# The last weight chunk of an MLP rounded ahead of the last relu: two buffers, two sums and one tile shape moved at the end of a transformer layer

## The chip, the cores and the metric

The kernel runs on one core of a Trainium2 chip. The metric is the time of one execution on the device in microseconds; the median of several runs is compared. The core's engines each work through a queue of their own: PE (matrix products; PEld is its loading of the stationary operand), DVE (elementwise, vector), ACT (elementwise, scalar), POOL, and SP, which here only issues transfers.

## The reference

One layer over a sequence of 256 rows of width 1024, in fp32: a gated sum of a convolution branch and a sparse attention branch, a cross attention over 256 memory rows, and a squared-relu MLP with hidden width 4096; then a last normalization. What the change touches is the MLP and the end:

```python
    hf = _rmsnorm(h, norm_ffn_g[l]) @ w_ff1[l]
    h = h + jnp.square(jax.nn.relu(hf)) @ w_ff2[l]
return _rmsnorm(h, norm_final_g)
```

## The kernel before

**Precision.** Each fp32 operand of a product is split into a rounded high part and a low part (`hi`, `lo`; of the hidden activations `fs` holds both), and a product is three matmuls: high by high, high by low, low by high (`mm3`). ACT makes the high part of a weight (`act(hi, raw)`, L254), DVE the low part (`raw - hi`, recorded under L79 as every DVE and PE instruction is, because a helper counts them).

**The stream of weights.** All weights come as chunks of 1 MB, in one order, into three rotating `raw` buffers, issued by SP. A chunk is rounded in two halves. Each half takes a slot of the pools `highs` and `lows`, six of each. The functions `split_high` and `split_low` take the next half off a list of jobs; `held` says how many slots stay free. `weights(...)` returns the parts of a half and counts its slot as used. Tiles of 8 KB per partition come from another rotation, `t8`, of 12 buffers. The name `raw66` means chunk 66 of the stream, `hi82_0` the high part of the first half of chunk 82.

**The MLP.** Both weight matrices are cut into 16 chunks of 256 hidden features, `f1` and `f2`. A turn c of the main loop computes both 128-feature tiles of hidden chunk c + 2 (`first`, into a bank `ps_f`), and between them adds chunk c to the output sums (`half_of`, `seventh`, into banks `ps_p`). There are 8 banks. Two are reserved for `ps_f`, but one of these holds a long-lived output sum, so that `ps_f` has a single bank: a new `first` waits until the last one's bank is read.

**Two tile shapes.** In a wide `first` a high weight part meets the high and low activations in one matmul of 512 columns, and the bank ends up with two halves that have to be added: ACT copies one (L396), DVE adds the other (`ft<-ps_f,ft`), ACT applies the relu and the square. A narrow `first` has three matmuls of 256 columns for each step instead; ACT's relu reads the bank directly (L1148), then comes the square (L1153). The turns in `SEVEN` are narrow, the other ones wide. After the square ACT makes the high part of the activations (L1172, `fs`) and DVE the low part.

**Seven banks.** For chunks 0 to 12 (`JOINED` = 13) the output products go through a scheme with seven sums, banks "1" to "7", which are combined into the residual `h_rm` at the end (`add_to` and the instructions on `comb`). Chunks 13 to 15 are multiplied in the ordinary way in `last_products`, which reuses the banks "2", "3", "1", "4", "5" in that order: first row block 0, both halves of the columns, then row block 1. Each is followed by the residual, squares and the last normalization, which scales and stores.

**Order.** The order of instructions in every queue is the order in which the Python code emits them. The end of the code after the loop: the last two parts of chunk 12 (`outer`, `inner`), the two tiles of hidden chunk 15, the weights of `f2` 13 to 15 (chunks 78 to 82 of the stream among others; 82 is `f2` 15, the last), the sums, the last products.

Of the kernel before, what the change touches and what calls it, by code (L numbers as in the profile page):

```python
# [9 lines left out]
F32R = mybir.dt.float32r  # L10
# [6 lines left out]
P = 128  # L17
# [38 lines left out]
N_CHUNK = KT * S  # L56
# [3 lines left out]
SEVEN = (2, 3, 4, 6, 7, 8, 10, 11, 12)  # L60
# [53 lines left out]
def block_kernel(ctx, tc, x, xt, mem, memt, wst, wki, vecs, convw, gout, out):  # L114
# [9 lines left out]
    highs = ctx.enter_context(tc.tile_pool(name="highs", bufs=HALVES))  # L124
    lows = ctx.enter_context(tc.tile_pool(name="lows", bufs=HALVES))
# [4 lines left out]
    def t8(name, dt=F32, shape=(P, KT, S)):  # L130
        return big.tile(list(shape), dt, tag="t8", bufs=12, name=name)

    def parts_t8(name, nkt=KT):
        return Parts([t8(f"{name}{c}", F32R, (P, 4, 2, S)) for c in range(nkt // 4)])

    def w2(name, dt=F32, shape=(P, 512)):
        return work.tile(list(shape), dt, tag="w2", bufs=8, name=name)
# [4 lines left out]
    def ps_mm(name):  # L142
        return bank("mm", 2, name)
# [12 lines left out]
        return (ps_mm if mm_turn[0] % 2 else ps_acc)(name)  # L156


    prepared, whole = {}, {}
    nload = [0]  # L160
    high_jobs, low_jobs = [], []

    def load(parts=1):
        if nload[0] >= len(STREAM):
            return
        c = nload[0]
        nload[0] += 1
        key = STREAM[c]
        raw = t8(f"raw{c}", F32, (P, N_CHUNK)) if c in EARLY else raws.tile([P, N_CHUNK], F32, tag="raw", name=f"raw{c}")
        n = KT * NK if key[0] == "ki" else N_CHUNK  # L170
        src = wki if key[0] == "ki" else wst[INDEX[key]]
        for q in range(parts):
            ns = slice(q * n // parts, (q + 1) * n // parts)
            nc.sync.dma_start(raw[:, ns], src[:, ns])
        if key in WHOLE:
            whole[key] = raw.rearrange("p (k n) -> p k n", k=2 * KT)
            return
        if key[0] == "f2" and key[1] in SEVEN:
            jobs = seven(key, c, raw)
        else:  # L180
            parts = 1 if key[0] == "ki" else 2
            jobs = []
            for q in range(parts):
                ns = slice(q * n // parts, (q + 1) * n // parts)
                jobs.append(Stage((*key, q), lambda ns=ns, q=q, last=q == parts - 1: high(key, c, raw, ns, q, last)))
        if key[0] == "f2" and key[1] < JOINED:

            at = [j.key for j in high_jobs].index(("f1", key[1] + 2, 1))
            first = len(jobs) // 2
            high_jobs[at:at] = jobs[:first]  # L190
            jobs = jobs[first:]
        if key == ("f1", JOINED + 2):

            at = [j.key for j in high_jobs].index(("f2", JOINED - 1, "inner"))
            high_jobs[at:at] = jobs[:1]
            jobs = jobs[1:]
        high_jobs.extend(jobs)

    class Stage:

        def __init__(self, key, high, before=None, slot=True):
            self.key, self.high, self.before, self.slot = key, high, before, slot

        def prepare(self):
            if self.before:
                self.before()
                self.before = None
# [41 lines left out]

    def high(key, c, raw, ns, q, last):  # L250
        n = ns.stop - ns.start
        hi = highs.tile([P, N_CHUNK // 2], F32R, tag="hi", name=f"hi{c}_{q}")[:, :n]
        lo = lows.tile([P, N_CHUNK // 2], F32R, tag="lo", name=f"lo{c}_{q}")[:, :n]
        act(hi, raw[:, ns], AF.Copy)  # L254

        def low():
            dve.tensor_tensor(out=lo, in0=raw[:, ns], in1=hi.bitcast(F32), op=ALU.subtract)
            prepared[(*key, q)] = (hi, lo)
            if last and c not in EARLY:
                load()  # L260

        low_jobs.append(low)

    def split_high():
        if high_jobs and (not high_jobs[0].slot or nsplit[0] - nused[0] < HALVES - held[0]):
            job = high_jobs.pop(0)
            nsplit[0] += job.slot
            job.prepare()
            job.high()

    def split_low():
        if low_jobs:
            low_jobs.pop(0)()
        if len(high_jobs) > 1:
            high_jobs[1].prepare()

    nsplit, nused, held = [0], [0], [1]

    def weights(kind, i, half, kt):

        key = (kind, i, half)
        while key not in prepared:
            split_high()
            split_low()
        nused[0] += half not in ("outer", "inner")
        return [w if kt is None else w.rearrange("p (k n) -> p k n", k=kt) for w in prepared.pop(key)]


# [6 lines left out]
    def add_some():  # L295
        if added and added[0][0] in ready and pe.total >= add_next[0]:
            pair, pause = added.pop(0)
            add_next[0] = pe.total + pause
            ready[pair]()
            if pair not in [p for p, _ in added]:  # L300
                held_back.append((pe.total + 10000, pair))
        if held_back and pe.total >= held_back[0][0]:
            fill.extend(queues.pop(held_back.pop(0)[1]))

    def split_ahead():
        split_low()
        split_high()

    def tick():
        for c in list(chains):  # L310
            if next(c, "end") == "end":
                chains.remove(c)
        while (len(fill) > 1 or (fill and (len(done) > 5 or nused[0] < 5))) and dve.total < pe.total - 1000:
            fill_one()
        dve.total = max(dve.total, pe.total - 2000)
        add_some()

    def fill_one():

        some = [q for q in fill[:3] if q is not turn[0]] or fill  # L320
        q = some[0] if len(some[0]) < 10 and len(fill) > 3 else max(some, key=len)
        turn[0] = q
        q.pop(0)()
        if not q:
            fill.remove(q)
# [99 lines left out]
    for parts in (2, 2, 1):  # L425
        load(parts)
# [8 lines left out]
    half = cst.tile([P, 2], F32, name="half")  # L435
# [336 lines left out]
    parts = (slice(0, P), slice(P, 3 * P))  # L772
# [42 lines left out]
    def qk(name):  # L815
        return big.tile([P, 2, S], F32, tag="qk", bufs=4, name=name)

    for i in range(4):
        q, k = qk(f"q{i}"), qk(f"k{i}")
# [275 lines left out]
    f2 = parts_t8("ff_p")  # L1095
# [112 lines left out]
    def product(name, a, w, j, cs=slice(0, 512)):  # L1208
        if name not in banks:
            banks[name] = {"2": ps_acc, "3": ps_acc, "4": ps_acc, "5": ps_acc, "7": ps_mm}.get(name, ps_aux)(f"ps_p{name}")  # L1210
        used[name] = used.get(name, 0) + 1
        mm3(banks[name], *a, w[0][:, j, cs], w[1][:, j, cs], used[name] == 1, used[name] == uses[name])
# [19 lines left out]
    def seventh(x, name):  # L1232
        w = weights("f2", x.c, name, None)
        split_ahead()
        for j, (bank_name, part) in enumerate(TERMS[name]):
            product(bank_name, x.of(part), w, j)

    def first(x, side, wide):
        ps = ps_mm(f"ps_f{x.c}{side}")
        w = weights("f1", x.c, side, KT)  # L1240
        split_ahead()
        tile_b(ps, w, f2, wide=wide)
        x.after(side, ps if wide else ps[:, :S])
        tick()
        if wide:
            tick()
# [4 lines left out]
    def by_tiles(ap):  # L1251
        return ap.rearrange("p (k f) -> p k f", f=P)
# [29 lines left out]
    def add_to(rb, hf, ps, scales):  # L1282
        h = h_rm[:, 4 * hf : 4 * hf + 4, rb, :]
        dve.scalar_tensor_tensor(out=h, in0=by_tiles(ps), scalar=scales[:, rb : rb + 1], in1=h, op0=ALU.mult, op1=ALU.add)

    for c in range(JOINED):
        hidden.append(Hidden(c + 2))
        x, later = hidden[c], hidden[c + 2]
        first(later, 0, c not in SEVEN)
        x.done()  # L1290
        if c in (0, 1, JOINED - 1):
            split_ahead()
        half_of(x, 0)
        first(later, 1, c not in SEVEN)
        if c < JOINED - 1:
            half_of(x, 1)
    hg = t8("hg", F32, (P, 2, D))
# [5 lines left out]
    r, b = r2[0], banks  # L1303
    minus = small.tile([P, 2], F32, tag="minus", name="minus")
    dve.tensor_scalar(minus, r, -1.0, None, ALU.mult)
    v, e, g = (w2(f"comb{j}") for j in range(3))
    act(v, b["1"], AF.Copy)
    add_to(0, 0, b["2"], r)
    seventh(x, "inner")
    tick()  # L1310
    first(hidden[-1], 1, False)
    held[0] = 0
    ws = {}
    for c in range(JOINED, 16):
        for k in range(2):
            ws[c, k] = weights("f2", c, k, 1)
            split_high()
            tick()
        hidden[c].done()

# [3 lines left out]
            mm3(ps, *hidden[c].row(k, rb), w[0][:, 0, cols], w[1][:, 0, cols], c == JOINED and k == 0,  # L1324
                c == 15 and k == 1)

    add_to(0, 0, v, r)
    add_to(0, 1, b["3"], r)
    dve.tensor_tensor(out=v, in0=b["6"], in1=v, op=ALU.subtract)
    dve.tensor_tensor(out=e, in0=b["5"], in1=v, op=ALU.add)  # L1330
    add_to(0, 1, e, r)
# [92 lines left out]
```

## Time and profile before

| what | value |
|---|---|
| median of 3 runs | 510.51 us (509.75 to 510.89) |
| profiled execution | 510.7 us, span 508.9 us |
| busy in the span | PE 496.6 us, DVE 456.3 us, ACT 348.6 us, POOL 31.6 us |
| mean granted clock of PE | 0.993 |
| largest groups in the chain that ended last | PE 71%, DVE 14%, ACT 5%, DMA 5% |

The profiled execution's own time is 1.8 us above its span. Starts in the rows are microseconds from the span's start. A row of the timeline has start, duration, engine, line, operation and tiles; "x2" joins rows that follow each other; in brackets stands how long the engine had been idle and what ended it. PE's durations overlap, since matmuls are pipelined: its pace is the distance between starts.

### The profile page before, as it was taken

To read this page: it belongs to the slowest core of one execution; us is meant where nothing else is said; L and a number is where in the kernel's file an instruction comes from. 1 tells how busy PE (TensorE), PEld (TensorE's weight loads), DVE (VectorE), ACT (ScalarE), POOL (GpSimd) and SP (SyncE) were. 2 spreads that over 40 slices of the span, in tenths; PEclk is the share of its full clock that TensorE was granted. 3 is DMA by queue.
4 is the path that set the end of the run, shared out by engine and by line. 5 is a ranking of instruction groups with operands and counts; after the bars stand their busy time and mean duration, and the time that the engine had idled before them with its cause. 6 is when DMAs were issued, how large, how long until landed. Compare 5 with 4: busy or idle time off the path is not lost.

```text
span 508.9 us, 8226 instructions
## 1 busy us (share of the span) xinstructions
PE 496.6 (98%) x3090; PEld 443.8 (87%) x3090; DVE 456.3 (90%) x855; ACT 348.6 (69%) x641; POOL 31.6 (6%) x49
## 2 busy tenths in 40 slices
PE   7999999999999999999999999999999999999984
PEld 6999998888888888888898999988988899899964
DVE  5999999999999799999899986799998999799693
ACT  7667777878666667678657666687777777677712
POOL 2002212311211000000000000000000000000000
PEclk9999999999999999999999999999999999999988
DMA  8959678899788524426645654446877445456302
GB/s 319 376 181 276 189 205 247 220 258 272 226 249 243 191 83 167 161 95 241 248 166 176 213 191 131 156 170 184 199 203 297 183 173 175 171 182 243 143 2 83
DMA packets 26649, 100.36 MB, mean 197 GB/s; under 512 B 10592, under 2 KB 11488, under 8 KB 16112
## 3 DMA queue, kind: packets, MB, share of 16 engines
q1 hardware_dynamic: 22544, 92.90, 52.9%
q0 software_dynamic: 3632, 6.59, 7.3%
q8 instruction: 24, 0.39, 0.3%
q10 hardware_dynamic: 432, 0.33, 0.2%
q14 instruction: 17, 0.14, 0.1%
HBM read 91.16 MB, written 1.05 MB: 181 GB/s over the span
## 4 chain that ended last, share of the span: by engine, by line
PE 71%; DVE 14%; ACT 5%; DMA 5%; issue 3%; SPq 0%; POOLq 0%; POOL 0%; DVEq 0%; ACTq 0%
PE ps_f L79 11%; PE ps_conv L79 9%; PE ps_p L79 7%; DMA raw<-in_wst_dram 5%; PE ps_ao L79 4%; PE ps_q L79 4%; PE ps_k L79 4%; PE ps_ga L79 4%; PE ps_gc L79 4%; DVE lo L79 4%; PE ps_v L79 4%; PE ps_xo L79 3%; PE ps_qi L79 2%; PE ps_xk L79 2%; PE ps_xv L79 2%
## 5 line engine op out<-in xcount | busy, mean ns | idle before, releaser
L79 DVE TENSOR_TENSOR lo<-raw,hi 128x1024 fp32r<-128x1024 f32 x145 | 175.7, 1216 | 5.8 <-ACT hi L254 5.7
L254 ACT ACTIVATE hi<-raw 128x1024 fp32r<-128x1024 f32 x145 | 150.7, 1046 | 3.2 <-DMA raw<-in_wst_dram 3.2
L79 PE MATMUL ps_f<-ff_p,hi 128*128 128x256 f32 (+1 forms) x416 | 92.9, 310 | 0.8 <-DVE ft L79 0.8
L79 DVE SCALAR_TENSOR_TENSOR acc<-u,cw,acc 128x234 f32<-128x234 f32 (+29 forms) x190 | 78.2, 464 | 0.3
L79 PEld LDWEIGHTS ps_f<-ff_p,hi 128*128 128x128 f32 x416 | 68.7, 191 | 7.2 <-DVE ft L79 1.6
L79 PE MATMUL ps_f<-ff_p,lo 128*128 128x256 f32 x256 | 70.2, 282 | 0.0
L79 PEld LDWEIGHTS ps_f<-ff_p,lo 128*128 128x128 f32 x256 | 48.7, 190 | 0.9
L79 PE MATMUL ps_conv<-n_p,hi 128*128 128x256 f32 x224 | 41.0, 285 | 0.0
L79 PE MATMUL ps_p<-hi,fs 128*128 128x512 f32 (+1 forms) x124 | 38.4, 381 | 0.6 <-DVE h_rm L79 0.6
L79 PEld LDWEIGHTS ps_conv<-n_p,hi 128*128 128x128 f32 x224 | 34.9, 192 | 0.8 <-issue 0.7
L79 PE MATMUL ps_conv<-n_p,lo 128*128 128x256 f32 x112 | 31.7, 283 | 0.0
L579 POOL DMA_DIRECT2D acc<-products x25 | 21.6, 864 | 122.3 <-ACT products L578 54.8
L79 PEld LDWEIGHTS ps_p<-hi,fs 128*128 128x128 f32 x124 | 23.3, 195 | 5.0 <-DVE h_rm L79 1.0
L79 PE MATMUL ps_p<-lo,fs 128*128 128x512 f32 (+1 forms) x62 | 23.8, 383 | 1.0 <-DVE lo L79 1.0
L79 PE MATMUL ps_q<-n_p,hi 128*128 128x512 f32 x64 | 23.6, 406 | 0.0
L79 PE MATMUL ps_k<-n_p,hi 128*128 128x512 f32 x64 | 23.5, 407 | 0.0
L79 PE MATMUL ps_ao<-o_p,hi 128*128 128x512 f32 x64 | 22.6, 401 | 0.0
L79 PE MATMUL ps_co<-u_p,hi 128*128 128x512 f32 (+1 forms) x80 | 22.2, 351 | 0.0
L79 PE MATMUL ps_mix<-mix_p,hi 128*128 128x512 f32 (+1 forms) x80 | 22.2, 351 | 0.0
L79 PE MATMUL ps_ga<-n_p,hi 128*128 128x512 f32 x64 | 22.0, 396 | 0.0
L79 PE MATMUL ps_gc<-n_p,hi 128*128 128x512 f32 x64 | 22.0, 396 | 0.0
L578 ACT ACTIVATE products<-u,cw 128x231 f32<-128x231 f32 (+24 forms) x50 | 21.9, 489 | 0.0
(370 smaller groups left out, 1194.6 us busy)
## 6 DMA issues: line engine op xcount, KB each, us to landing
raw<-in_wst_dram SPq DMA_DIRECT2D x80, 1024.0 KB, 5.0
acc<-products POOLq DMA_DIRECT2D x25, 256.0 KB, 5.6
raw<-in_wst_dram SPq DMA_DIRECT2D x4, 512.0 KB, 7.3
x_rm<-in_x_dram SPq DMA_DIRECT2D x2, 512.0 KB, 4.1
mem_rm<-in_mem_dram SPq DMA_DIRECT2D x1, 1024.0 KB, 9.1
mem_t<-in_memt_dram SPq DMA_DIRECT2D x1, 1024.0 KB, 11.0
h_t<-in_xt_dram SPq DMA_DIRECT2D x1, 1024.0 KB, 7.1
h_rm<-turned SPq DMA_DIRECT2D x16, 64.0 KB, 7.0
```

The lines of the kernel that those rows point to most:

```text
L79: return fn(*args, **kwargs)
L254: act(hi, raw[:, ns], AF.Copy)
L578: act(prod[:, a, s:], u[:, t, : S - s], AF.Copy, scale=cw[:, t, TAPS - 1 - s : TAPS - s])
L579: nc.gpsimd.dma_start(acc[:, ts, :], prod, accum_op=ALU.add)
```

## The change

Three edits, all in the MLP.

1. The two halves of the last chunk (`f2` 15) no longer take slots: high and low part of a half share one `t8` tile, `both82_0` and `both82_1`. With that the limit `held` needs no lifting, and two calls of `split_ahead` before the last `first` round them earlier.
2. Of the sums that combine the seven banks, two move up: the one of bank "3" and the one of `v`, the copy of bank "1", are added to `h_rm` before the last `first` is emitted.
3. Turn 5 of the main loop uses narrow tiles (hidden chunk 7).

```diff
-                jobs.append(Stage((*key, q), lambda ...: high(key, c, raw, ns, q, last)))
+                jobs.append(Stage((*key, q), lambda ...: high(key, c, raw, ns, q, last),
+                                  slot=key != ("f2", 15)))
...
+            if not slot:
+                elsewhere.add(key)
...
-        hi = highs.tile([P, N_CHUNK // 2], F32R, tag="hi", name=f"hi{c}_{q}")[:, :n]
-        lo = lows.tile([P, N_CHUNK // 2], F32R, tag="lo", name=f"lo{c}_{q}")[:, :n]
+        if (*key, q) in elsewhere:
+            both = t8(f"both{c}_{q}", F32R, (P, 2, n))
+            hi, lo = both[:, 0, :], both[:, 1, :]
+        else:
+            hi = highs.tile([P, N_CHUNK // 2], F32R, tag="hi", name=f"hi{c}_{q}")[:, :n]
+            lo = lows.tile([P, N_CHUNK // 2], F32R, tag="lo", name=f"lo{c}_{q}")[:, :n]
...
-        nused[0] += half not in ("outer", "inner")
+        nused[0] += key not in elsewhere
...
-        first(later, 0, c not in SEVEN)
+        wide = c not in SEVEN and c != 5
+        first(later, 0, wide)
...
-        first(later, 1, c not in SEVEN)
+        first(later, 1, wide)
...
     add_to(0, 0, b["2"], r)
     seventh(x, "inner")
+    add_to(0, 1, b["3"], r)
+    split_ahead()
     tick()
+    add_to(0, 0, v, r)
+    split_ahead()
     first(hidden[-1], 1, False)
-    held[0] = 0
     ws = {}
     for c in range(JOINED, 16):
         for k in range(2):
             ws[c, k] = weights("f2", c, k, 1)
-            split_high()
             tick()
...
-    add_to(0, 0, v, r)
-    add_to(0, 1, b["3"], r)
```

What it does to the queues shows at three places. ACT at the end, before, with what each instruction waits for: `comb0` is `v`, `ft15` and `fs15` are the last hidden chunk, `ps_f151` its second tile.

```order
L1307 ACTIVATE comb0_5354<-ps_p1_4117 128x512
L1172 ACTIVATE fs15_5307<-ft15_5308 128x256 [waits Activation_49]
L254 ACTIVATE hi82_0_5368<-raw82_5266 128x1024 [waits DMAHW5_49,DVE_49]
L1148 ACTIVATE ft15_5308<-ps_f151_5367 128x256 [waits PE_49]
L1153 ACTIVATE ft15_5308<-ft15_5308 128x256 [waits Activation_49]
L254 ACTIVATE hi82_1_5398<-raw82_5266 128x1024 [waits DVE_49]
L1172 ACTIVATE fs15_5307<-ft15_5308 128x256 [waits Activation_49]
```

And now:

```order
L1315 ACTIVATE comb0_5366<-ps_p1_4117 128x512
L261 ACTIVATE both82_0_5372<-raw82_5278 128x1024 [waits DMAHW5_49]
L261 ACTIVATE both82_1_5382<-raw82_5278 128x1024
L1179 ACTIVATE fs15_5319<-ft15_5320 128x256 [waits Activation_49]
L1155 ACTIVATE ft15_5320<-ps_f151_5387 128x256 [waits PE_49]
L1160 ACTIVATE ft15_5320<-ft15_5320 128x256 [waits Activation_49]
L1179 ACTIVATE fs15_5319<-ft15_5320 128x256 [waits Activation_49]
```

Both high parts of chunk 82 stand ahead of the last relu, and neither waits for DVE; the second one stood between the last square and the last `fs`.

DVE at the same place, before: `ps_p2` is bank "2", `lo81_1` the low part of the half before the last two.

```order
L79 SCALAR_TENSOR_TENSOR h_rm<-ps_p_3880,ms_ff,h_rm 128x4x128
L79 TENSOR_TENSOR lo_1_5323<-raw_5253,hi_1_5322 128x1024
L79 TENSOR_TENSOR fs_5307<-ft_5308,fs_5307 128x256 x2
L79 TENSOR_TENSOR lo_0_5369<-raw_5266,hi_0_5368 128x1024
L79 TENSOR_TENSOR lo_1_5399<-raw_5266,hi_1_5398 128x1024
L79 SCALAR_TENSOR_TENSOR h_rm<-comb_5354,ms_ff,h_rm 128x4x128
L79 SCALAR_TENSOR_TENSOR h_rm<-ps_p_3903,ms_ff,h_rm 128x4x128
L79 TENSOR_TENSOR comb_5354<-ps_p_4196,comb_5354 128x512
```

And now:

```order
L79 SCALAR_TENSOR_TENSOR h_rm<-ps_p_3880,ms_ff,h_rm 128x4x128
L79 TENSOR_TENSOR lo_1_5335<-raw_5265,hi_1_5334 128x1024
L79 SCALAR_TENSOR_TENSOR h_rm<-ps_p_3903,ms_ff,h_rm 128x4x128
L79 TENSOR_TENSOR both_0_5372<-raw_5278,both_0_5372 128x1024
L79 SCALAR_TENSOR_TENSOR h_rm<-comb_5366,ms_ff,h_rm 128x4x128
L79 TENSOR_TENSOR both_1_5382<-raw_5278,both_1_5382 128x1024
L79 TENSOR_TENSOR fs_5319<-ft_5320,fs_5319 128x256 x2
L79 TENSOR_TENSOR comb_5366<-ps_p_4196,comb_5366 128x512
```

Four instructions, two low parts and two sums, moved from behind the last two `fs` to ahead of them; the rest keeps its order.

ACT in turn 5, before: `ft7` and `fs7` are hidden chunk 7, `ps_f70` and `ps_f71` its two tiles.

```order
L235 ACTIVATE hi66left_4446<-raw66_4411 128x1024
L396 ACTIVATE ft7_4443<-ps_f70_4444 128x256
L235 ACTIVATE hi66last_4468<-raw66_4411 128x512
L1152 ACTIVATE ft7_4443<-ft7_4443 128x256
L1153 ACTIVATE ft7_4443<-ft7_4443 128x256
```

And now:

```order
L238 ACTIVATE hi66left_4446<-raw66_4411 128x1024
L1155 ACTIVATE ft7_4443<-ps_f70_4444 128x256
L1160 ACTIVATE ft7_4443<-ft7_4443 128x256
L238 ACTIVATE hi66last_4476<-raw66_4411 128x512
L1179 ACTIVATE fs7_4442<-ft7_4443 128x128
```

The relu now reads the bank itself, at the place where the copy stood, behind `hi66left`; on DVE the two instructions `ft7<-ps_f..,ft7` of turn 5 are gone. The transfers that SP issues keep their order.

More of the change, by code (lines that the diff above doesn't have):

```diff
@@ L156, in ps_turn @@
         return (ps_mm if mm_turn[0] % 2 else ps_acc)(name)
-    prepared, whole = {}, {}
+    prepared, whole, elsewhere = {}, {}, set()
     nload = [0]
@@ L184, in load @@
                 ns = slice(q * n // parts, (q + 1) * n // parts)
-                jobs.append(Stage((*key, q), lambda ns=ns, q=q, last=q == parts - 1: high(key, c, raw, ns, q, last)))
+                jobs.append(Stage((*key, q), lambda ns=ns, q=q, last=q == parts - 1: high(key, c, raw, ns, q, last),
+                                  slot=key != ("f2", 15)))
         if key[0] == "f2" and key[1] < JOINED:
```

## The prediction

> **What bounds the kernel now.** I read the page's busy table first, then the windows by stage, then the waits of the last 65 us, and then the timeline at each place where PE idles. The page and two windows:
>
> ```profile
> PE 496.6 (98%) x3090; PEld 443.8 (87%) x3090; DVE 456.3 (90%) x855; ACT 348.6 (69%) x641; POOL 31.6 (6%) x49
> PEclk9999999999999999999999999999999999999988
> ...
> 406.00:477.00 71.00, 71.00 (x455) 64.41 (x454) 66.63 (x90) 53.24 (x87) 0.00 (x0) 1.00 0.55 200
> ...
> 488.00:491.50 3.50, 3.50 (x10) 2.68 (x10) 3.40 (x6) 0.00 (x0) 0.00 (x0) 0.54 0.02 5
> ```
>
> A window's first column after the bounds is its length, then follow busy time of PE, PEld, DVE, ACT, POOL, the granted clock, and DMA. From 406 to 477 us PE has no idle time at all, so what is gained before 406 is kept to 477 if no new wait opens. From 488 to 491.5 PE looks busy but was granted a clock of 0.54. The waits from 445 us on that lie near this:
>
> ```profile
> DVE fs L79 <- ACT fs L1172: 5.0, 2, 4.3
> ...
> PE ps_p L79 <- DVE lo L79: 1.0, 2, 0.8
> ...
> PE ps_p L79 <- DVE h_rm L79: 0.6, 1, 0.6
> ```
>
> DVE idles 4.3 us in one piece, and right after that PE waits for DVE three times. The timelines of ACT, DVE and PE there:
>
> ```profile
> 478.00 0.58 ACT L1307 ACTIVATE comb<-ps_p 128x512 f32<-128x512 f32 x1
> ...
> 481.52 0.38 ACT L1148 ACTIVATE ft<-ps_f 128x256 f32<-128x256 f32 x1 [1.69 <-PE ps_f L79]
> 481.93 0.42 ACT L1153 ACTIVATE ft<-ft 128x256 f32<-128x256 f32 x1
> 482.26 1.04 ACT L254 ACTIVATE hi<-raw 128x1024 fp32r<-128x1024 f32 x1
> 483.21 0.40 ACT L1172 ACTIVATE fs<-ft 128x256 fp32r<-128x256 f32 x1
> ```
>
> ```profile
> 477.03 1.21 DVE L79 TENSOR_TENSOR lo<-raw,hi 128x1024 fp32r<-128x1024 f32 x1
> ...
> 483.64 0.43 DVE L79 TENSOR_TENSOR fs<-ft,fs 128x256 fp32r<-128x256 f32 x1 [4.30 <-ACT fs L1172]
> 483.98 2.35 DVE L79 TENSOR_TENSOR lo<-raw,hi 128x1024 fp32r<-128x1024 f32 x2
> 486.25 0.74 DVE L79 SCALAR_TENSOR_TENSOR h_rm<-comb,ms_ff,h_rm 128x512 f32<-128x512 f32 x1
> 486.91 0.74 DVE L79 SCALAR_TENSOR_TENSOR h_rm<-ps_p,ms_ff,h_rm 128x512 f32<-128x512 f32 x1
> 487.57 1.41 DVE L79 TENSOR_TENSOR comb<-ps_p,comb 128x512 f32<-128x512 f32 x2
> ...
> 493.12 0.75 DVE L79 SCALAR_TENSOR_TENSOR h_rm<-ps_p,ms_ff,h_rm 128x512 f32<-128x512 f32 x1
> ...
> 496.87 0.72 DVE L79 TENSOR_SCALAR hg<-hg,rs_o 128x352 f32<-128x352 f32 x2 [0.66 <-POOL rs_o L1272]
> 497.79 0.75 DVE L79 SCALAR_TENSOR_TENSOR h_rm<-ps_p,ms_ff,h_rm 128x512 f32<-128x512 f32 x1 [0.21 <-PE ps_p L79]
> ```
>
> ```profile
> 481.32 0.40 PE L79 MATMUL ps_p<-hi,fs 128*128 128x512 f32 x1
> ...
> 485.25 0.50 PE L79 MATMUL ps_p<-lo,fs 128*128 128x512 f32 x1 [0.80 <-DVE lo L79]
> ...
> 486.38 0.50 PE L79 MATMUL ps_p<-lo,fs 128*128 128x512 f32 x1 [0.17 <-DVE lo L79]
> ...
> 487.71 0.73 PE L79 MATMUL ps_p<-hi,fs 128*128 128x512 f32 x1 [0.59 <-DVE h_rm L79]
> ...
> 491.69 0.39 PE L79 MATMUL ps_p<-lo,fs 128*128 128x512 f32 x1
> ...
> 497.14 0.39 PE L79 MATMUL ps_p<-lo,fs 128*128 128x512 f32 x1
> ```
>
> Bank "2" takes 18 matmuls from 481.32 on: the 14th waits for the low part of the last chunk's first half (485.25), the 17th for that of its second half (486.38). Bank "3" starts only when its old content has been added to `h_rm` (487.71). Behind these gaps comes the half clock. DVE's last row shows that the end hangs on PE: DVE waits there for bank "1".
>
> **The end, step by step.** In steady pace the row at 491.69 (bank "3", 11th matmul) and the one at 497.14 (bank "1", 17th) are 24 matmuls apart: 5.45 / 24 = 0.227 us each. The row at 491.69 is 28 matmuls behind 481.32, which would take 28 x 0.227 = 6.36 us without a wait and at full clock, that is 487.68. So 491.69 - 487.68 = 4.0 us can be had, if every operand is there in time.
>
> ACT: behind the copy `v` (478.00 + 0.58) come both high parts, 1.04 each, to 480.7, and the first `fs`, 0.40, to 481.1. The last relu is released by PE at 481.52, so it is not delayed. Its square ends at 482.35 as before; the last `fs` follows at once and ends at about 482.8 instead of 483.6.
>
> DVE: the low part that starts at 477.03 ends at 478.2; the sum of bank "3" takes 0.66 (486.25 to 486.91) and ends at 478.9. The first low part has to wait for its high part, 479.6, and at 2.35 / 2 = 1.18 ends at 480.8. The sum of `v` ends at 481.5, the second low part at 482.7, the two `fs` at 0.34 to 0.43 each at 483.5. So the 4.30 us of idle time cover both low parts and both sums. PE needs the low parts at its 14th and 17th matmul, 481.32 + 13 x 0.227 = 484.27 and 484.95, the last `fs` at its 18th, 485.18, and bank "3" at 485.41. They stand ready at 480.8, 482.7, 483.5 and 478.9. The smallest margin is 1.7 us, so I take the three stalls as gone.
>
> What is late next: DVE's other sums now start at 483.5 instead of 487.57 and reach the first residual after 493.12 - 487.57 = 5.55 us, at 489.0. PE has bank "2" ready by then, so the DVE sets the pace for row block 0: from 493.12 to 496.87 + 0.72 are 4.5 us, so it is through at 493.5. Bank "1" is ready at 497.79 - 4.0 = 493.8. That leaves 0.3 us. Were DVE a microsecond later than this, 0.7 us of the 4.0 would be lost. The bank reads go to banks that PE does not write then.
>
> The clock: I count its drop to the stalls. The 3.41 us before it hold 1.85 us of PE work (columns: length, PE busy with its count, clock, DMA):
>
> ```profile
> 484.30:487.71 3.41, 1.85 (x6) 1.00 0.01 2
> ```
>
> Without the drop the eight matmuls from 487.71 to about 491.2 take 8 x 0.227 = 1.8 us, so 1.7 of the 4.0 us are clock and 2.3 are waits. The Trainium skill ("TensorE: Matmul & The Clock Gate", "Why this matters for your kernels") says that idle gaps over about 3 us, or one whole window of idle, put the clock at half. The longest gap here is 0.8 us; by the rule as worded the stalls did not cause the drop, and removing them would gain 2.3 instead of 4.0. I take the trace: no other stretch of the MLP is so empty, and none has the drop.
>
> The other edits here: the `t8` tiles and the counting cost no instruction. SP keeps its order, and no transfer is added. The last chunk's transfer is done when ACT comes to it at 478.6 instead of 478.8:
>
> ```profile
> 477.00:478.00 1.00, 1.00 (x7) 0.82 (x7) 1.00 (x2) 0.71 (x3) 0.00 (x0) 1.00 0.00 0
> ```
>
> The DMA share is nothing from 477 on, a margin of 1.6 us.
>
> **Turn 5.** The only real PE stall between 390 and 477 us is here:
>
> ```profile
> 393.35 1.06 ACT L235 ACTIVATE hi66left<-raw 128x1024 fp32r<-128x1024 f32 x1 [2.12 <-DMA raw<-in_wst_dram]
> 394.31 0.36 ACT L396 ACTIVATE ft<-ps_f 128x256 f32<-128x256 f32 x1
> ```
>
> ```profile
> 394.71 0.42 DVE L79 TENSOR_TENSOR ft<-ps_f,ft 128x256 f32<-128x256 f32 x1 [1.90 <-ACT ft L396]
> ...
> 437.72 0.42 DVE L79 TENSOR_TENSOR ft<-ps_f,ft 128x256 f32<-128x256 f32 x1 [2.10 <-ACT ft L396]
> ```
>
> ```profile
> 394.01 0.39 PE L79 MATMUL ps_p<-hi,fs 128*128 128x512 f32 x1
> 395.19 0.50 PE L79 MATMUL ps_f<-ff_p,hi 128*128 128x512 f32 x1 [0.79 <-DVE ft L79]
> ...
> 400.85 0.40 PE L79 MATMUL ps_f<-ff_p,hi 128*128 128x256 f32 x2
> ...
> 403.73 0.40 PE L79 MATMUL ps_p<-hi66left,fs 128*128 128x512 f32 x1
> ...
> 432.53 0.39 PE L79 MATMUL ps_f<-ff_p,hi 128*128 128x512 f32 x1
> ...
> 435.35 0.40 PE L79 MATMUL ps_p<-hi,fs 128*128 128x512 f32 x1
> ...
> 438.20 0.50 PE L79 MATMUL ps_f<-ff_p,hi 128*128 128x512 f32 x1
> ```
>
> ACT stands at `hi66left` until a transfer lands, the copy queues behind it, the DVE sum behind that, and PE waits for the bank: ready one pace of 0.23 after 394.01, at 394.24, it starts at 395.19. With the narrow form the bank is free at the end of the relu, which takes the copy's place: 394.31 + 0.38 + the 0.06 that PE needed behind the DVE sum = 394.75, so 0.44 earlier. A narrow tile takes 403.73 - 400.85 = 2.88, a wide one 435.35 - 432.53 = 2.82. Of the two additions of 0.06 the first lies inside the wait, the second counts: net -0.4 us. The two DVE sums that go (0.42 each) and two of ACT's copies gain nothing directly, since PE binds. Bounds: with the transfer early enough that nobody waits, the edit only costs 2 x 0.06 = +0.1; if the relu did not have to wait at all, the gain would be 0.95 - 0.1 = 0.8.
>
> What is late next: turn 9, wide still, has the same pattern, and PE starts there at 438.20, 0.06 behind the end of the DVE sum. If chunk 74 does not land earlier, the 0.4 is lost there. But its transfer is issued when DVE has read the chunk before it, and DVE, fed by ACT and PE, comes earlier too; so I keep it.
>
> **Sum.** -4.0 - 0.4 = -4.4 us against the profiled 510.70: 506.3. The median of the runs is 0.2 lower, so 506.1 for a median.
>
> **Rivals.**
> - The clock drops anyway, by the skill's rule above or because the window that decides is set by something else: 1.7 us are not gained, 507.8. For it: I have one drop only. Against it: it follows at once on the emptiest stretch. 8%.
> - Turn 5 gains nothing, because turn 9 takes it back or the transfer lands earlier: 506.5 to 506.6. 10%, inside my range.
> - The last chunk's parts don't come earlier, because the `t8` buffers are held, so that only turn 5 counts: 510.1. Against it: in the order the first `both` waits for a transfer alone and the second for nothing. 3%.
> - Slower: the last transfer lands late. Both high parts now stand in ACT's queue ahead of the last relu. A landing up to 479.0 costs nothing there, since the relu waits for PE till 481.52; up to about 480.7 the margin of 1.7 us at PE's 18th matmul absorbs it; behind that each microsecond costs one, and from 485 on the whole gain is gone. The landing before 477 speaks against it. 511.6 or more; 2%, with 2% more for what I don't see.
> - The forecast as summed: 75%.
>
> The range reaches up to the clock rival with the spread of the runs, 508.0, and down to the full gain in turn 5 (506.1 - 0.4 = 505.7) less a spread of 0.7, 505.0. About 0.2%, 1 us, is what a measurement of this kernel can tell from no change. Faster by more: the forecast, the clock rival and turn 5's, 0.93; within: 0.04, the held buffers and part of the unseen; slower: 0.03.
>
> **What the next profile should show.** PE without a wait from 481 us to its last matmul and a clock of 1.00 there; DVE's 4.3 us of idle time gone, about 0.7 left (waiting for the first high part); the last relu still waiting for PE; the first residual of row block 0 at about 488.6 and bank "1"'s at 493.4 with DVE nearly busy in between; in turn 5 a PE wait of about 0.4 us on ACT's relu. I am wrong if the clock row shows a drop again, if PE waits for `both`, or if DVE, not PE, releases bank "1"'s residual.

## The result and the profile after

The changed kernel takes 506.46 us (506.22 to 507.13, 6 runs) against 509.87 us (509.64 to 510.89, 6 runs): ratio 0.9931, 95% [0.9918, 0.9944]. Run again later it took 506.63 us (506.18 to 507.32), ratio 0.9933 [0.9910, 0.9956]. The forecast was 506.1 us, within 505.0 to 508.0; the gain is 3.4 us where 4.4 were forecast. The profiled execution took 506.91 us.

The page of the changed kernel, and four windows with the columns as before:

```profile
span 505.1 us, 8254 instructions
...
PE 494.5 (98%) x3106; PEld 444.7 (88%) x3106; DVE 455.6 (90%) x853; ACT 348.2 (69%) x639; POOL 31.7 (6%) x49
...
PEclk9999999999999999999999999999999999999999
```

```profile
481.30:487.70 6.40, 6.40 (x32) 5.32 (x31) 6.29 (x11) 1.22 (x3) 0.00 (x0) 1.00 0.00 1
488.00:491.50 3.50, 3.50 (x17) 2.89 (x16) 3.43 (x7) 1.14 (x3) 0.00 (x0) 1.00 0.00 0
390.00:406.00 16.00, 15.60 (x102) 13.94 (x101) 13.38 (x20) 10.27 (x17) 0.00 (x0) 1.00 0.66 239
406.00:477.00 71.00, 71.00 (x455) 64.68 (x454) 66.55 (x90) 53.30 (x87) 0.00 (x0) 1.00 0.55 198
```

Where the window from 488 held 10 matmuls at a clock of 0.54, it now holds 17 at 1.00, and the stretch of the three stalls is full. The timelines of ACT, DVE and PE at the end:

```profile
478.67 2.00 ACT L261 ACTIVATE both<-raw 128x1024 fp32r<-128x1024 f32 x2
480.57 0.40 ACT L1179 ACTIVATE fs<-ft 128x256 fp32r<-128x256 f32 x1
481.71 0.38 ACT L1155 ACTIVATE ft<-ps_f 128x256 f32<-128x256 f32 x1 [0.74 <-PE ps_f L79]
...
482.58 0.42 ACT L1179 ACTIVATE fs<-ft 128x256 fp32r<-128x256 f32 x1
```

```profile
478.35 0.74 DVE L79 SCALAR_TENSOR_TENSOR h_rm<-ps_p,ms_ff,h_rm 128x512 f32<-128x512 f32 x1
479.75 1.23 DVE L79 TENSOR_TENSOR both<-raw,both 128x1024 fp32r<-128x1024 f32 x1 [0.66 <-ACT both L261]
...
481.56 1.22 DVE L79 TENSOR_TENSOR both<-raw,both 128x1024 fp32r<-128x1024 f32 x1
482.69 0.76 DVE L79 TENSOR_TENSOR fs<-ft,fs 128x256 fp32r<-128x256 f32 x2
...
488.92 0.75 DVE L79 SCALAR_TENSOR_TENSOR h_rm<-ps_p,ms_ff,h_rm 128x512 f32<-128x512 f32 x1
...
492.67 0.72 DVE L79 TENSOR_SCALAR hg<-hg,rs_o 128x352 f32<-128x352 f32 x2 [0.66 <-POOL rs_o L1279]
493.98 0.75 DVE L79 SCALAR_TENSOR_TENSOR h_rm<-ps_p,ms_ff,h_rm 128x512 f32<-128x512 f32 x1 [0.59 <-PE ps_p L79]
```

```profile
481.51 0.40 PE L79 MATMUL ps_p<-hi,fs 128*128 128x512 f32 x1
...
484.26 1.52 PE L79 MATMUL ps_p<-both,fs 128*128 128x512 f32 x6
485.62 0.39 PE L79 MATMUL ps_p<-hi,fs 128*128 128x512 f32 x1
```

DVE's 4.30 us of idle time are 0.66, the last relu still waits for PE, the last six matmuls of bank "2" run in one piece, and bank "3" follows 0.23 behind the last of them. Bank "1"'s residual (493.98) is released by PE.

Counted from bank "2"'s first matmul to the end of the span, the stretch was 508.9 - 481.32 = 27.58 us and is 505.1 - 481.51 = 23.59 us: 4.0 us, as forecast (spans are printed to a tenth). The other 0.2 us of later start are the remainder of 0.7 us that the unchanged part ahead of turn 5 ran late in this execution.

In turn 5 the relu reads the bank at the copy's place, and PE waits for it:

```profile
394.17 1.06 ACT L238 ACTIVATE hi66left<-raw 128x1024 fp32r<-128x1024 f32 x1 [2.15 <-DMA raw<-in_wst_dram]
395.13 0.36 ACT L1155 ACTIVATE ft<-ps_f 128x256 f32<-128x256 f32 x1
```

```profile
395.55 0.50 PE L79 MATMUL ps_f<-ff_p,hi 128*128 128x256 f32 x2 [0.40 <-ACT ft L1155]
```

### The profile page after: what moved, and what is told of

The parts are those of the page before. It is cut to its first block, busy times and chain, and to the rows that moved or that the text cites. A ratio compares the mean times of both kernels' runs of the same rounds, so it can differ in the third digit from the quotient of the medians.

```text
span 505.1 us, 8254 instructions
## 1 busy us (share of the span) xinstructions
PE 494.5 (98%) x3106; PEld 444.7 (88%) x3106; DVE 455.6 (90%) x853; ACT 348.2 (69%) x639; POOL 31.7 (6%) x49
## 4 chain that ended last, share of the span: by engine, by line
PE 71%; DVE 14%; ACT 5%; DMA 5%; issue 3%; POOLq 0%; POOL 0%; DVEq 0%; ACTq 0%; SPq 0%
PE ps_f L79 10%; PE ps_conv L79 10%; PE ps_p L79 7%; PE ps_ao L79 4%; PE ps_q L79 4%; PE ps_k L79 4%; PE ps_ga L79 4%; PE ps_gc L79 4%; PE ps_v L79 4%; DMA raw<-in_wst_dram 4%; DVE lo L79 4%; PE ps_xo L79 3%; PE ps_qi L79 2%; PE ps_xk L79 2%; PE ps_xv L79 2%
## 5 line engine op out<-in xcount | busy, mean ns | idle before, releaser
L79 DVE TENSOR_TENSOR lo<-raw,hi 128x1024 fp32r<-128x1024 f32 x143 | 173.1, 1215 | 6.3 <-ACT hi L261 6.0
L261 ACT ACTIVATE hi<-raw 128x1024 fp32r<-128x1024 f32 x143 | 148.7, 1046 | 2.8 <-DMA raw<-in_wst_dram 2.8
L79 PEld LDWEIGHTS ps_f<-ff_p,hi 128*128 128x128 f32 x432 | 70.8, 191 | 6.3 <-ACT ft L1155 1.9
L79 PE MATMUL ps_p<-hi,fs 128*128 128x512 f32 (+1 forms) x104 | 32.5, 375 | 0.0
L79 PEld LDWEIGHTS ps_p<-hi,fs 128*128 128x128 f32 x104 | 19.2, 188 | 3.2
L79 PEld LDWEIGHTS ps_conv<-n_p,lo 128*128 128x128 f32 x112 | 21.5, 192 | 0.0
```

What stands on the lines that cost most here:

```text
L79: return fn(*args, **kwargs)
```

## The experiments

**One part at a time.** Four kernels. The first keeps turn 5 wide:

```diff
-        wide = c not in SEVEN and c != 5
+        wide = c not in SEVEN
```

> The changed kernel with turn 5 wide again: the two edits at the end alone. My theory: three stalls of PE, 2.3 us, and the half clock behind them, 1.7 us, both go, so 4.0 us under the kernel before, and the profile shows PE without a wait from the first matmul of bank 2 to the last one and a clock of 1.00. Rival, the drop of the clock has nothing to do with the stalls: 2.3 us and a row with a half clock. Rival, what was measured short of the forecast (3.4 instead of 4.4 us) is missing here: 3.0 us.

Measured: 506.89 us (506.48 to 507.81), 0.9940 [0.9919, 0.9961], against 509.51 us for the kernel before: 3.1 us by the ratio, the last rival's number and not the 4.0 of my theory, though the trace shows what the theory said (table below). The second is the kernel before with turn 5 narrow and nothing else:

```diff
-        first(later, 0, c not in SEVEN)
+        wide = c not in SEVEN and c != 5
+        first(later, 0, wide)
```

> The kernel before with turn 5 narrow alone. My theory: 0.4 us under the kernel before, since PE waits in turn 5 for the relu's end and no longer for the DVE sum behind the copy; at the end the waits of 0.80, 0.17 and 0.59 us and the half clock stand as they were. Rival, the shortfall of the forecast is here and turn 9 or a later wait takes the gain back: no difference, or 0.1 us more. The times can hardly tell these two apart, so the profile is to be read: distance from the first matmul of turn 5 to the first one of bank 2 at the end, 92.64 us before and 92.14 us in the changed kernel.

Measured: 509.15 us (508.68 to 510.13), 0.9985 [0.9972, 0.9999], a difference too small to decide by time (the same kernel against itself gives 1.0022 below). The third has the early parts, but both sums at their old place and turn 5 wide:

```diff
-    add_to(0, 1, b["3"], r)
     split_ahead()
     tick()
-    add_to(0, 0, v, r)
     split_ahead()
...
+    add_to(0, 0, v, r)
+    add_to(0, 1, b["3"], r)
```

> The kernel with the last chunk's parts in buffers of their own and early, but with the two sums at their old place behind the last fs, and turn 5 wide. My theory: the sums of v and of bank 3 then end near 484.5 us, 0.9 us before bank 3 is needed, so PE does not wait; DVE reaches row block 0 about 1.1 us later than with the sums moved, which the waits at the end (0.59, 0.68 and 1.21 us for PE) absorb: 4.0 us under the kernel before, the same as with the sums moved. Rival, the sums are what frees bank 3 in time: PE waits there again for h_rm, and 0.7 us or more of the 4.0 is not gained.

Measured: 507.42 us (507.10 to 508.20), 0.9950 [0.9929, 0.9970]: 2.6 us by the ratio, where 4.0 was expected. The fourth is the kernel before with only the two sums moved:

```diff
     seventh(x, "inner")
+    add_to(0, 1, b["3"], r)
     tick()
+    add_to(0, 0, v, r)
```

> The kernel before with the two sums moved alone; the last chunk's parts are made as late as before. My theory: the waits of PE's 14th and 17th matmul of bank 2 stand (0.80 and 0.17 us in the rows, 0.95 and 0.33 us against the steady pace); the wait for h_rm goes, so PE is 0.8 us earlier at bank 3. If the clock drops as before the gain is 0.8 us; if the drop needs all three stalls it goes too and the gain is about 2.4 us.

Measured: 508.49 us (507.76 to 509.21), 0.9972 [0.9958, 0.9985]: 1.4 us by the ratio, between the two expected gains, with all twelve executions at a mean clock of 0.996 to 0.998. What the traces of all these show, with the kernel before and the changed one repeated (waits of PE in us; the stretch is from bank "2"'s first matmul to the end of the span):

| kernel | wait in turn 5 | wait in turn 9 | waits at the end | clock behind them | stretch |
|---|---|---|---|---|---|
| before | 0.79 | none | 0.80, 0.17, 0.59 | half for 3.41 us | 27.58 |
| before, repeated | 0.71 | 1.02 | 0.80, 0.17, 0.59 | full | 26.04 |
| changed | 0.40 | none | none | full | 23.59 |
| changed, repeated | 0.22 | none | none | full | 23.55 |
| tail alone | 0.90 | 0.73 | none | full | 23.57 |
| turn 5 alone | 0.16 | none | 0.80, 0.17, 0.59 | half for 3.41 us | 27.55 |
| parts alone | 1.0 | none | none | full | 23.61 |
| sums alone | 0.80 | none | 0.80, 0.16 | full | 25.12 |

Five of these traces also have a wait of 0.18 to 0.60 us in turn 4, at 383 us, and one has 0.40 us at 373.

So in the traces the early parts make the whole gain of the end by themselves; with them DVE is early enough for the sums in either place. By the medians the parts alone are 0.5 us slower than the whole tail (507.42 against 506.89); the stretch at the end does not hold this, and its cause stays open. The sums alone remove the third wait. The gains of 4.0 us were missed in the medians because the kernel before does not always lose the clock:

> The kernel before, for a trace of an execution without the drop, if the profiled one is such, and for more clocks. Theory: the three waits of bank "2" and bank "3" (0.80, 0.17, 0.59 us) stand as in the first trace, but with the clock at 1.00 from bank "2" to the end are 27.58 - 1.7 = 25.9 us. Times in two groups again: about 509.2 us at 0.995 to 0.998 and about 511 us at 0.993. If the waits differ where the clock differs, the two groups are something else.

Measured: 510.92 us (12 runs), 1.0022 [1.0003, 1.0041] against the same kernel beside it, which is the size of difference that means nothing here. The profiled execution, of 510.24 us, is one without the drop. Its timeline of PE and its windows:

```profile
482.46 0.40 PE L79 MATMUL ps_p<-hi,fs 128*128 128x512 f32 x1
...
486.40 0.50 PE L79 MATMUL ps_p<-lo,fs 128*128 128x512 f32 x1 [0.80 <-DVE lo L79]
...
487.53 0.51 PE L79 MATMUL ps_p<-lo,fs 128*128 128x512 f32 x1 [0.17 <-DVE lo L79]
...
488.86 0.50 PE L79 MATMUL ps_p<-hi,fs 128*128 128x512 f32 x1 [0.59 <-DVE h_rm L79]
```

```profile
483.37:486.78 3.41, 2.61 (x12) 1.84 (x11) 2.00 (x3) 1.38 (x3) 0.00 (x0) 1.00 0.01 2
486.78:490.20 3.42, 2.66 (x11) 1.56 (x10) 3.35 (x6) 0.00 (x0) 0.00 (x0) 1.00 0.03 5
```

The waits are the same to the hundredth, the clock stays at 1.00, and the stretch is 1.5 us shorter. In the kernel before, 14 of 60 executions on the chip that ran most of these experiments had a mean clock of 0.993, as the profiled one; their median is about 511.2 us, that of the others 509.4, and the two groups overlap (510.5 to 511.9 and 508.7 to 511.5 us). The mean lies below 1.00 without a drop too: after the last matmuls the clock is at half again (0.50 from 503.06 us on in the profile of the changed kernel). All 12 of the changed kernel lie at 0.996 to 0.998.

Turn 9 also varies. In the repeated kernel before, the pattern of turn 5 stands there:

```profile
437.53 1.06 ACT L235 ACTIVATE hi74left<-raw 128x1024 fp32r<-128x1024 f32 x1 [2.30 <-DMA raw<-in_wst_dram]
438.49 0.36 ACT L396 ACTIVATE ft<-ps_f 128x256 f32<-128x256 f32 x1
```

```profile
439.37 0.50 PE L79 MATMUL ps_f<-ff_p,hi 128*128 128x512 f32 x1 [1.02 <-DVE ft L79]
```

With turn 5 wide it cost 0.7 to 1.0 us in two traces of five; with turn 5 narrow PE was busy for 71.00 of the 71 us from 406 in all three traces of the table and in five more of the kernels below.

**What drops the clock.** Into the changed kernel I put DVE additions ahead of the second low part, to make one wait of a chosen length in bank "2". In the traces it falls on the 15th matmul, the first that takes the low part of the last hidden chunk (`fs`):

```diff
     add_to(0, 0, v, r)
+    for j in range(5):          # 5, 6 or 9
+        dve.tensor_tensor(out=hg[:, j % 2, 0:512], in0=g_out[0], in1=g_out[1], op=ALU.add)
     split_ahead()
```

> The changed kernel with five additions of 128x512 by DVE (two banks of results that are added and overwritten later) put ahead of the second low part of the last chunk, so that PE stalls once in bank "2". By the rows of before an addition of this size takes 0.62 to 0.68 us of DVE; the slack of the last fs is 1.7 us, so the stall is about 5 x 0.66 - 1.7 = 1.6 to 1.8 us. Theory A (the clock is decided by how much PE works in a fixed window of 3.41 us, wherever the window happens to lie; 1.85 of 3.41 us before gave a drop, 2.44 of 3.41 with the sums alone gave none): the drop comes in some executions and not in others; 506.5 + 1.7 = 508.2 us at a mean clock of 0.997 or so without it, 509.9 at 0.993 to 0.994 with it. Theory B (the prediction's: every stall of this size brings the drop): 509.9 in all. Theory C (only an idle time over some 3 us brings it, the rule of the Trainium skill, TensorE: Matmul & The Clock Gate, Why this matters for your kernels): 508.2 in all.

Measured: 508.24 us (507.52 to 509.05), all ten executions at 0.995 to 0.998: no drop, where theory A had some and theory B, the prediction's, had one in each, so that theory B is out. The wait:

```profile
485.22 1.20 PE L79 MATMUL ps_p<-both,fs 128*128 128x512 f32 x4 [1.30 <-DVE fs L79]
```

The middle wait, run after the other two:

> As the short and the long stall, with six additions: with five PE was idle for 1.30 us and no execution of 10 had a drop of the clock; with nine it was idle for 3.71 us and all of 11 lost about 1.4 us more than the stall or had a lower clock. Six make about 1.30 + 0.62 = 1.9 us. Theory A (the idle time within a window of 3.41 us at a place that is chance, the drop from about 1.3 to 1.6 us on, as the three gaps of before, 1.56 us spread over 3.3 us, give a drop in about a quarter of its executions): a drop in more than half of the executions but not in all, since the window can cut the gap: 508.9 us without it, 510.6 us with it. Theory C (one idle time of some 3 us): no drop, 508.9 us in all.

Measured: 508.77 us (508.06 to 511.94): seven executions at 0.995 to 0.998 with 508.1 to 508.9 us, five at 0.992 or 0.993 with 509.9 to 511.9 us. The profiled one kept its clock:

```profile
485.76 1.20 PE L79 MATMUL ps_p<-both,fs 128*128 128x512 f32 x4 [1.90 <-DVE fs L79]
```

So an idle time of some 3 us is not needed, which theory C held. The long wait:

> As the short stall, with nine additions instead of five: the stall is about 9 x 0.66 - 1.7 = 4.2 to 4.4 us. Theory A: wherever the window of 3.41 us lies, one of them holds at most about 1.3 us of PE work, so the drop comes in every execution: 506.5 + 4.3 + 1.7 = 512.5 us, mean clock 0.993 or lower. Theory C says the same here. If the clock never drops with a single stall, however long: 510.8.

Measured: 512.17 us (511.53 to 513.39), mean clocks 0.989 to 0.995, and every execution at least 1.0 us above 506.63 + 3.87, the delay of the matmul that waits (484.35 by its pace, 488.22). Two executions at 0.995 can't be told by their clock, as kernels without a drop reach that too; two at 0.989 and 0.990, of 513.4 us, may have had a second window at half clock, which no trace shows. The drop in the windows of the profiled one:

```profile
482.87:486.28 3.41, 1.64 (x8) 1.02 (x6) 3.41 (x7) 0.00 (x0) 0.00 (x0) 1.00 0.00 0
486.29:489.70 3.41, 1.48 (x6) 1.24 (x7) 3.38 (x6) 0.00 (x0) 0.00 (x0) 1.00 0.00 0
489.70:493.11 3.41, 3.41 (x9) 2.64 (x8) 3.34 (x6) 0.00 (x0) 0.00 (x0) 0.50 0.00 0
```

Why just these bounds: a trace also records the clock by intervals. In the three traces with a drop here it lasts 3.413 us and begins 481.28 us, that is 141 x 3.4133, behind the first entry of that record (6.53 us in the kernel before, 8.42 in the long wait). The fall to half after the last matmuls lies on the same grid in all 14 traces, 145 or 146 windows behind the first entry. I cut the traces on that grid and took 0.227 us of work for each matmul from its start on (0.12 for the narrow ones), cut off at the edges of the window:

| execution | window | PE work in it, us | clock behind it |
|---|---|---|---|
| before | 484.40 to 487.81 | 1.24 | half |
| turn 5 alone | 483.83 to 487.25 | 1.25 | half |
| long wait | 486.29 to 489.70 | 1.36 | half |
| long wait | 482.87 to 486.29 | 1.48 | full |
| sums alone | 483.24 to 486.65 | 2.01 | full |
| short wait | 481.75 to 485.16 | 2.03 | full |
| before, repeated | 483.37 to 486.78; 486.78 to 490.20 | 2.35; 2.08 | full |
| middle wait | 481.57 to 484.99; 484.99 to 488.40 | 2.14; 2.52 | full |

So in these traces the clock is set for one window by the work in the one before, on a grid that the program does not set, and the bound lies between 1.36 and 1.48 us of work in 3.41. From the first entry on, no window of the 14 traces breaks this: the emptiest other one with full clock behind it holds about 1.4 us (at the kernel's start, with matmuls of other shapes at their own pace), and those at the kernel's end with half clock behind them at most 1.0. The bare number of starts does not separate the windows; there are six in each of the first four.

By this bound a wait has to take about 3.41 - 1.4 = 2.0 us of work out of one window. The short wait puts its matmul 1.5 us behind its pace, too little wherever the grid lies. The middle one puts it 2.1 us behind, enough only where nearly all of it lies in one window: by estimate in (3.41 - 2.1 + 0.2) / 3.41 = 0.44 of the executions, and 5 of 12 had the drop. So theory A held in kind, and its sizes did not. The Trainium skill ("TensorE: Matmul & The Clock Gate", "What's actually happening") states such a free-running window of 3413 ns, and the traces agree. Its wording that a gap over about 3 us, or a whole idle window, halves the clock ("Why this matters for your kernels", as the prediction cites it) is too narrow for this case: 0.80, 0.17 and 0.59 us within one window were enough.

**Beyond the change.** In turn 5 ACT still stands at `hi66left` ahead of the relu. I emitted its rounding behind the relu and the square of that tile:

```diff
+        late = side == 0 and x.c in LATE       # (7,): the tile of turn 5
-        split_ahead()
+        if late: split_low()
+        else: split_ahead()
         tile_b(ps, w, f2, wide=wide)
...
         tick()
+        if late: split_high()
```

> The changed kernel with one thing more: in turn 5 the rounding of the half chunk hi66left, which waits for a transfer in ACT's queue, is emitted behind the relu and the square of that turn's first tile instead of ahead of them. Theory: PE's wait for that relu (0.40 us, 0.55 us behind its pace) goes, and turn 9 keeps it: 506.46 - 0.5 = 506.0 us. Rival: hi66left then comes late for the products or turn 9's wait opens again, which its profile would show at 438 us: 506.5. Rival: the relu moves ahead, but the low part and with it DVE's queue fall behind: 507.

Measured: 505.82 us (505.58 to 506.57), 0.9919 [0.9898, 0.9940]. The wait in turn 5 is gone, turn 9 has none, and one of 0.64 us is left in turn 4. ACT in turn 5:

```profile
392.34 0.38 ACT L1156 ACTIVATE ft<-ps_f 128x256 f32<-128x256 f32 x1 [0.52 <-PE ps_f L80]
392.75 0.42 ACT L1161 ACTIVATE ft<-ft 128x256 f32<-128x256 f32 x1
394.10 1.06 ACT L239 ACTIVATE hi66left<-raw 128x1024 fp32r<-128x1024 f32 x1 [0.93 <-DMA raw<-in_wst_dram]
```

The changed kernel itself, on the same chip beside it:

> The changed kernel once more, beside the three others on the same chip, for the spread of its times and clocks. If the drop of the clock is a thing of the kernel before alone: all of its executions at a mean clock of 0.995 to 0.998, 506.3 to 507.1 us, while those of before fall into two groups, about 509.2 us at 0.995 to 0.998 and about 511 us at 0.993.

Measured: 506.63 us, so the late rounding is worth 0.8 us by the medians. Then in every turn:

```diff
-LATE = (7,)
+LATE = tuple(range(2, 15))
```

> The late rounding of turn 5 in every turn: the half that used to be rounded ahead of a turn's first relu is rounded behind that relu and its square. In the run with turn 5 alone, one PE wait was left, 0.64 us at 383.5 us, where ACT waited for the sum of a chunk (inner) ahead of a relu. Theory: that wait goes, others of its kind with it: 505.8 - 0.5 = 505.3 us. Rival: a half that is rounded later by a relu and a square (0.36 + 0.42 us, and its low part with it) is late for its product in some turn, so that a wait comes back elsewhere: 505.8 to 507 us.

Measured: 509.10 us (508.61 to 509.51), 0.9974 [0.9952, 0.9997]: by the ratios 2.8 us behind the version with turn 5 alone. Waits came back, as the rival said, but not because a part was late for its product. ACT, DVE and PE ahead of the first of three new waits:

```profile
361.94 0.63 ACT L1180 ACTIVATE fs<-fn 128x512 fp32r<-128x512 f32 x1 [2.85 <-DVE fn L80]
...
363.20 1.04 ACT L239 ACTIVATE inner<-sums 128x1024 fp32r<-128x1024 f32 x1
...
371.66 0.64 ACT L1180 ACTIVATE fs<-fn 128x512 fp32r<-128x512 f32 x1 [2.84 <-DVE fn L80]
...
373.15 0.36 ACT L1156 ACTIVATE ft<-ps_f 128x256 f32<-128x256 f32 x1
```

```profile
364.27 1.22 DVE L80 TENSOR_TENSOR inner<-sums,inner 128x1024 fp32r<-128x1024 f32 x1 [2.37 <-ACT inner L239]
...
370.56 0.42 DVE L80 TENSOR_TENSOR fn<-ft 128x256 f32<-128x256 f32 x1
```

```profile
373.56 0.51 PE L80 MATMUL ps_f<-ff_p,hi 128*128 128x256 f32 x2 [0.97 <-ACT ft L1156]
```

The same places of ACT and DVE with turn 5 alone:

```profile
358.46 1.06 ACT L239 ACTIVATE inner<-sums 128x1024 fp32r<-128x1024 f32 x1 [1.18 <-DVE sums L80]
...
360.58 0.63 ACT L1180 ACTIVATE fs<-fn 128x512 fp32r<-128x512 f32 x1 [0.75 <-DVE fn L80]
```

```profile
360.46 1.22 DVE L80 TENSOR_TENSOR inner<-sums,inner 128x1024 fp32r<-128x1024 f32 x1
...
367.13 0.42 DVE L80 TENSOR_TENSOR fn<-ft 128x256 f32<-128x256 f32 x1
```

`inner`, the rounding of one of the sums of the seven-bank scheme, used to stand ahead of `fs<-fn`, in time in which ACT waits for DVE. Now it stands behind the relu, which itself stands behind `fs<-fn` and its wait of 2.85 us. DVE, whose instructions come in the same order in both kernels, stands idle for 2.37 us until `inner` is made. It reaches the next `fn` 3.4 us later than with turn 5 alone (370.56 against 367.13; 1.4 of them it was behind already), ACT waits for that, and the relu comes late for PE.

Last, turns 4 and 5 only. DVE's order is the same here too, so it is not what sets this kernel apart, as the next text has it:

```diff
-LATE = (7,)
+LATE = (6, 7)
```

> The late rounding in turns 4 and 5 only. In every turn it lost 3.3 us, since DVE then had other work ahead of what ACT waits for in turns 2 and 3; with turn 5 alone one PE wait was left, 0.64 us at 383.5 us, in turn 4, where ACT waits for DVE's sums ahead of a relu. In turn 4 the change moves one instruction of ACT (the high part of inner) behind a relu and its square, and nothing in DVE's order. Theory: that wait goes, and 505.8 - 0.2 to 0.6 = 505.2 to 505.6 us, as the wait was 0.2 to 0.6 us in the traces. Rival: inner comes later by 0.36 + 0.42 us and its low part with it, so that the wait comes back behind it: 505.8 us.

Measured: 505.44 us (505.17 to 505.74), 0.9917 [0.9902, 0.9932], the fastest here and below both kernels; its trace lists no wait of PE from 300 us to the end. In turn 4 `inner` is not delayed: it starts at 381.68 us, against 382.16 with turn 5 alone. From turn 5 alone (0.9919) the ratios don't separate it.

## Why the prediction was right, and where it was off

- **The stalls at the end: right.** With the 0.19 us of later start taken off, the first low part ended at 480.8 (forecast 480.8), the second at 482.6 (482.7), the `fs` at 483.3 (483.5), bank "3"'s sum at 478.9 (478.9). The first residual came at 488.7 (489.0). Row block 0 was through at 493.2 (493.5), bank "1" ready at 493.8 (493.8), and DVE waited 0.59 us for it where 0.3 was forecast. The tail alone and the parts alone show it without turn 5. One margin was misread: the low part of the first `fs` is needed at the 15th matmul, so that by the prediction's own figures the smallest margin is 481.32 + 14 x 0.227 - 483.1 = 1.4 us, not the 1.7 at the 18th. It was not used up, but the added waits fell on that matmul.
- **The two sums: costed together with the parts, and not needed.** The parts alone give the same stretch, 23.61 against 23.59.
- **The clock: the mechanism right, the term mis-sized against the median.** The stalls caused the drop, as I held against the Trainium skill's wording: without them no execution of the changed kernel (12), of the tail alone (6) or of the parts alone (7) had a mean clock below 0.995. But they do not bring it each time, and "1.7 of the 4.0 us are clock" holds only for an execution that has the drop, about one in four. In the others the stretch falls from 26.04 to 23.59, 2.45 us (forecast for the stalls: 2.3). The drop itself cost 27.58 - 26.04 = 1.54 us. That the two profiled stretches differ by just the 4.0 forecast is in part luck: the stalls were worth a little more, the drop a little less, and the profiled execution happened to have one.
- **From the profile to the median: the step that failed.** I took 0.2 us off because the median lay that much lower, as though the profiled execution were an ordinary one. It had the drop (about 1.5 us too long) and no wait in turn 9 (up to 1 us too short); the two partly cancelled in its time, but not in the gain. The time itself came closer (506.46 against 506.1) because the kernel before, in six runs, was at 509.87 us and not at the 510.51 of three.
- **Turn 5: right.** From the start of the turn to its second tile the five traces with wide tiles take 6.43 to 6.68 us, on average 6.55; the two of the changed kernel take 6.18 and 6.00, turn 5 alone 5.94: 0.4 to 0.6 earlier (forecast 0.44). To the start of turn 6, with the longer narrow tile, 0.3 to 0.5 are left (forecast 0.4). PE's wait on the relu was 0.40 and 0.22 us in the changed kernel, 0.16 in turn 5 alone (0.4). Turn 9 did not take it back, and in executions where turn 9 waits the edit seems to save that too. The saving in turn 9 is seen in the traces only, not isolated by a kernel of its own.
- **The sum for a median, as the runs show it:** 2.45 for the stalls, 0.3 to 0.5 in turn 5, some part of the 1 us of turn 9 and of the 1.5 us of clock: 2.8 to 3.0 plus those parts, against 3.4 measured.
- **Rivals.** The clock did not drop in any execution of the changed kernel. The `t8` buffers held nothing up, and the last transfer was there when ACT came (478.67, directly behind the copy `v`).

## What to carry to other kernels

Ahead of the last dependent step, give work that waits for nothing its own buffers and put it into the idle time that the step leaves on its engines; count the margin at each consumer. A gain read off one profiled execution has to be split into what every execution loses and what only some lose; a mean clock per run and a second profile show which is which. In a queue that runs in order, a rounding that waits for a transfer belongs behind the short instruction that PE waits for, but not where that instruction stands behind a wait of its own: then the engine that needs the rounding stands idle too.

## What the runs showed of the hardware that was not expected

- One half-clock window of 3.41 us costs this kernel 1.5 us, and no single long idle gap is needed: three gaps of 1.56 us together did it in about a quarter of the executions (14 of 60), one of 1.30 us in 0 of 10, one of 1.90 us in 5 of 12.
- PE's busy column does not sort these windows: 1.85 us busy came before a drop and 1.64 did not. Nor does the number of starts, six in both. The work from each start on, at the steady pace and cut at the edges of the window, does: 1.36 us and less before a drop, 1.48 us and more without one in the windows of the table.
